# A two-layer diffusion transformer on one core: modulation weights by half tiles over two queues, and layer 1's output product on float16 parts

## The chip, the core and the metric

The kernel runs on one core of a Trainium2 chip as one launch. Its time is the device time of an execution in microseconds (us), and the figure for the kernel before is the median of three runs, 1782.79 us (1778.72 to 1785.88). All five engines are used: TensorE (PE, with its weight loads shown as PEld), VectorE (DVE), ScalarE (ACT), GpSimd (POOL) and SyncE (SP), whose only work here is to issue DMAs. POOL issues DMAs too.

## What is computed

Two layers work on 256 tokens of width 2048 and, in layer 0, on 256 context tokens as well. Layer 0 mixes with a two-dimensional Fourier transform, layer 1 with windowed attention (64 query heads, 8 key heads, context keys in front). Around each branch stands an adaptive normalisation whose shift, scale and gate come from one vector:

```python
for i in range(DEPTH):
    shift, scale, gate = jnp.split((jax.nn.silu(c) @ ada_w[i] + ada_b[i])[:, None, :], 3, axis=-1)
    h = _rmsnorm(x, norm_g[i]) * (1 + scale) + shift
    ...
    y = ...                       # 256 x 4096: Fourier branch, or attention, times silu(z)
    x = x + gate * (y @ w_out[i]) # the output product: 4096 x 2048 weights
    if need_ctx:
        xc = xc + gate_c * (yc @ w_out[i])
return _rmsnorm(x, final_g)
```

Inputs and output are float32. Each operand of a product is split into a high and a low part, and the product is three matmuls.

## The kernel before

**Products.** `mm3` (L144 to L147) issues high times high, high times low and low times high into one bank of PSUM. There are two ways to make the parts. `split` (L65 to L67) copies to float32r on ACT (`S.copy`, L66) and subtracts on DVE (L67); `half_split` does that for half a 1 MB weight tile, and needs two buffers of the pool `ws` (six buffers of 4 KB a partition), one for each part. `split16` (L133 to L138) scales by a power of two into float16 on ACT (L137) and makes the rest on DVE (L138); both parts share one `ws` buffer. The power of two comes from the sum of squares of the whole operand, and is divided out behind the product.

**Order.** Every engine has its own instruction queue and works through it in order. A scheduler puts the instructions of each engine in order when the program is built; `tc.issue_after(x)` tells it that what stands inside must come behind x in that engine's queue. A tile of a pool can be written only when all who use the buffer's earlier tile are done.

**The stages around the change.**
- *z products of layer 0* (about 330 to 670 us): 32 blocks. Beside them run side jobs. `ada_jobs` (L767 on) computes the modulation vectors on DVE with multiply-and-sum instructions over the modulation weights `adw` (L796, each 128x1024, two of them for each half tile, one for layer 1's gate); there are 64 tiles of 1 MB, taken one at a time by `next(ada)`. In this stage each is loaded as two halves, one into `zr` (two buffers) by SP's queue and one into `wa` (a `ws` buffer) by POOL's. `scan_loads` and `scan_sums` (L815 to L825) load layer 0's output weights a first time, in 128x512 pieces by POOL's queue into the pool `act` (33 buffers), and sum their squares on ACT (L817).
- *Output product of layer 0* (about 670 to 1000 us): `for i in range(32)`, two sweeps of 16 steps over 1 MB tiles of `wo0`; a step is 2 weight halves x 8 blocks x 3 = 48 matmuls of 128x512. Steps with kg < 14 use float16 parts. `y_split0` (L868 to L884) makes the float16 parts of y two k at a time: ACT L882, DVE L883. Its output tiles come from the pool `y`, whose 32 buffers hold the 32 y themselves, except the first, which is an `act` tile; so the parts of y number k go into the buffer of y number k-1. In this stage the modulation tiles (38 are left) are loaded whole, into the pool `raw` (three buffers) and by SP's queue, like the tiles of `wo0`. `ada_rate` says how many a step takes: one, two in steps 6 to 9 and 17 to 24, none in 14 to 16 and from 29 on.
- *Keys and values of layer 1* (about 1005 to 1094 us): 8 steps of 48 matmuls on float32r.
- *Attention* (about 1095 to 1620 us): 66 slots (L1430 on). A slot issues the scores of a head pair (`stage_s`: four matmuls, L1359 and L1360; DVE's maximum L1361, ACT's exponential L1364, the float16 probabilities L1376 and L1377, then a DMA transpose by SP's queue), the values of two slots earlier (`stage_o`, L1394 and L1395) and two "units" of projection work from a list: 64 of queries, 64 of z, and at last 12 units ("o") of layer 1's output product, two k-steps each for the first 512 columns. A unit's weights are split one unit ahead. The rotary embedding and some subtractions run on POOL. `y_split` (L1180) splits y for the output product: ACT casts 256 columns, POOL subtracts for k < 24 and DVE for the rest; the parts lie in the 16 buffers of the pool `h1`, which hold the normalised input until the last z unit has read it, and in `act` tiles.
- *The rest of layer 1's output product* (about 1620 to 1770 us): columns 512 to 1535 from `wo1b` and 1536 to 2047 from `wo1c`, all on float32r parts, then gate, residual and the final norm.

Layer 1's output product has 32 k-steps; for each, two token blocks x four chunks of 512 columns x 3 matmuls.

## Time and profile before

| | |
|---|---|
| median of three runs | 1782.79 us (1778.72 to 1785.88) |
| the profiled execution | 1780.77 us |
| its span, first to last instruction | 1779.0 us |
| mean granted TensorE clock | 0.997 |
| HBM read / written | 391.91 MB / 12.59 MB |

The execution that was profiled lies 2.02 us under the median, and 1.77 us of it lie outside the span. In a timeline row the columns are start, length, engine, line and operation, out<-in, and in brackets how long the engine had been idle and what ended that. A row of a group of instructions has count, total, mean length in ns, and then the idle time in front of them. A row of stretches gives, for each, the busy time and the number of instructions of every engine, then the granted clock, the busy share of the 16 DMA engines and GB/s. Matmuls overlap: a row shows one as 0.38 or 0.40 us long, and the pace is the distance between starts.

### The profile page before, as it was taken

To read this page: it belongs to the slowest core of one execution; us is meant where nothing else is said; L and a number is where in the kernel's file an instruction comes from. 1 tells how busy PE (TensorE), PEld (TensorE's weight loads), DVE (VectorE), ACT (ScalarE), POOL (GpSimd) and SP (SyncE) were. 2 spreads that over 40 slices of the span, in tenths; PEclk is the share of its full clock that TensorE was granted. 3 is DMA by queue.
4 is the path that set the end of the run, shared out by engine and by line. 5 is a ranking of instruction groups with operands and counts; after the bars stand their busy time and mean duration, and the time that the engine had idled before them with its cause. 6 is when DMAs were issued, how large, how long until landed. Compare 5 with 4: busy or idle time off the path is not lost. (4 is left out here: it accounts for less than half of the span.)

```text
span 1779.0 us, 26403 instructions
## 1 busy us (share of the span) xinstructions
PE 1740.9 (98%) x9517; PEld 1222.3 (69%) x9517; DVE 1392.8 (78%) x2401; ACT 1062.4 (60%) x1989; POOL 293.3 (16%) x368
## 2 busy tenths in 40 slices
PE   6999999999999999999999999999999999999997
PEld 4679999544444444446444888788878888887886
DVE  5779888797777778876885654899899999997455
ACT  5545556377767747544122533688788878896343
POOL 0002111212222132000000000412303230233010
PEclk9999999999999999999999999999999999999999
DMA  9998998778988989774775323588998897987543
GB/s 394 417 357 247 283 276 237 296 285 319 328 305 317 313 302 322 262 298 171 284 287 222 119 95 115 169 193 208 213 209 199 222 217 203 206 210 264 191 167 142
DMA packets 220962, 438.74 MB, mean 247 GB/s; under 512 B 154720, under 2 KB 155120, under 8 KB 189088
## 3 DMA queue, kind: packets, MB, share of 16 engines
q1 hardware_dynamic: 182784, 351.85, 61.0%
q0 software_dynamic: 33904, 78.25, 14.8%
q10 hardware_dynamic: 4144, 6.95, 1.1%
q8 instruction: 75, 1.23, 0.3%
q14 instruction: 55, 0.45, 0.1%
HBM read 391.91 MB, written 12.59 MB: 227 GB/s over the span
## 5 line engine op out<-in xcount | busy, mean ns | idle before, releaser
L67 DVE TENSOR_TENSOR wl<-raw,wh 128x1024 fp32r<-128x1024 f32 x213 | 282.0, 1329 | 144.5 <-ACT wh L66 129.8
L66 ACT CAST wh<-raw 128x1024 fp32r<-128x1024 f32 x213 | 222.4, 1045 | 177.4 <-PE ps L146 152.7
L146 PE MATMUL ps<-act,wf 128*128 128x512 f16 x512 | 194.0, 379 | 0.0
L145 PE MATMUL ps<-act,wf 128*128 128x512 f16 x512 | 189.8, 379 | 1.4 <-ACT act L864 0.7
L147 PE MATMUL ps<-act,wf 128*128 128x512 f16 x512 | 191.1, 379 | 0.0
L1323 PE MATMUL ps<-h,wh 128*128 128x512 f32 x512 | 184.8, 396 | 0.0
L145 PEld LDWEIGHTS <-wf 128*128 128x128 f16 x960 | 94.0, 98 | 118.0 <-ACT wf L137 7.9
L145 PE MATMUL ps<-y,wf 128*128 128x512 f16 x448 | 170.3, 381 | 3.5 <-ACT wf L137 3.5
L147 PEld LDWEIGHTS <-wf 128*128 128x128 f16 x960 | 93.9, 98 | 113.2 <-DVE wf L138 0.3
L146 PE MATMUL ps<-y,wf 128*128 128x512 f16 x448 | 170.8, 381 | 0.0
L146 PEld LDWEIGHTS <-wf 128*128 128x128 f16 x960 | 94.1, 98 | 109.5 <-issue 1.1
L147 PE MATMUL ps<-y,wf 128*128 128x512 f16 x448 | 164.4, 379 | 0.0
L137 ACT ACTIVATE wf<-raw,nrm 128x1024 f16<-128x1024 f32 x56 | 61.3, 1140 | 139.3 <-DMA raw<-in_wo 133.9
L1325 PE MATMUL ps<-h,wl 128*128 128x256 f32 x512 | 138.6, 281 | 0.0
L146 PE MATMUL ps<-wl,h 128*128 128x512 f32 x320 | 126.8, 396 | 0.2 <-DVE wl L67 0.2
L147 PE MATMUL ps<-wh,h 128*128 128x512 f32 x320 | 125.3, 395 | 0.0
L145 PE MATMUL ps<-wh,h 128*128 128x512 f32 x320 | 124.0, 402 | 0.0
L138 DVE SCALAR_TENSOR_TENSOR wf<-raw,tn,wf 128x1024 f16<-128x1024 f32 x64 | 79.8, 1282 | 42.5 <-ACT wf L137 42.4
L1377 DVE SCALAR_TENSOR_TENSOR f<-p,sm,f 128x512 f16<-128x512 f32 x128 | 105.7, 845 | 9.0 <-ACT f L1376 8.6
L1323 PEld LDWEIGHTS ps<-h,wh 128*128 128x128 f32 x512 | 96.3, 188 | 19.0
L1364 ACT ACTIVATE p<-ps,mx 128x512 f32<-128x512 f32 x128 | 87.9, 689 | 35.4 <-DVE mx L1361 30.6
L1376 ACT ACTIVATE f<-p,sm 128x512 f16<-128x512 f32 x128 | 87.6, 717 | 31.8 <-DMA ft<-f 12.9
(394 smaller groups left out, 4452.1 us busy)
## 6 DMA issues: line engine op xcount, KB each, us to landing
raw<-in_wz SPq DMA_DIRECT2D x64, 1024.0 KB, 5.4
raw<-in_adw SPq DMA_DIRECT2D x38, 1024.0 KB, 6.3
raw<-in_awp SPq DMA_DIRECT2D x32, 1024.0 KB, 12.7
act<-in_wo POOLq DMA_DIRECT2D x128, 256.0 KB, 7.2
raw<-in_wo SPq DMA_DIRECT2D x32, 1024.0 KB, 6.7
raw<-in_wq SPq DMA_DIRECT2D x32, 1024.0 KB, 5.2
raw<-in_wu SPq DMA_DIRECT2D x32, 1016.0 KB, 6.6
raw<-in_wo1b SPq DMA_DIRECT2D x16, 1024.0 KB, 4.9
```

Of the source, the lines that this page charges most:

```text
L66: last_cast[0] = S.copy(h, src).ins
L67: last_sub[0] = eng.tensor_tensor(l, src, h.bitcast(F32), op=ALU.subtract).ins
L137: last_cast[0] = S.activation(w[:, 0], src, AF.Copy, scale=up).ins
L138: last_sub[0] = V.scalar_tensor_tensor(w[:, 1], src, up, w[:, 0], op0=ALU.mult, op1=ALU.subtract).ins
L145: PE.matmul(o, wh, xh, start=start, stop=False)
L146: PE.matmul(o, wh, xl, start=False, stop=False)
L147: return PE.matmul(o, wl, xh, start=False, stop=stop).ins
L1323: PE.matmul(o[0], wh[:, q], hx1[k], start=k == 0, stop=k == KT - 1)
L1325: PE.matmul(o[0][:, 0:N], wl[:, q], hx1[k][:, 0:N], start=False, stop=False)
L1364: S.activation(pt[tb], so[tb], AF.Exp, bias=mx[:, tb : tb + 1], scale=-1.0, accum_out=sm[:, tb : tb + 1])
L1376: S.activation(f[:, 0:512], pt[tb], AF.Copy, scale=sm[:, tb : tb + 1])
L1377: V.scalar_tensor_tensor(f[:, 512:1024], pt[tb], sm[:, tb : tb + 1], f[:, 0:512], op0=ALU.mult, op1=ALU.subtract)
```

## The change

It has four parts, and what each does to the instruction queues is told behind the diff.

```diff
 # ada_jobs
-                            if f == 0 and not out0[0]:
+                            if f == 0:
                                 wf = adat.tile([P, 1024], F32, tag="zr", name="zr", bufs=2)
                                 nc.sync.dma_start(wf, a["adw"][i, kh, fg][:, q])
-                            elif not out0[0]:
+                            else:
                                 wf = wsp.tile([P, 1024], F32, tag="ws", name="wa")
                                 nc.gpsimd.dma_start(wf, a["adw"][i, kh, fg][:, q])
-                            else:
-                                if f == 0:
-                                    w = raw(a["adw"][i, kh, fg])
-                                wf = w[:, q]
 # layer 0's output product
-                        t = (ypool if k else actp).tile([P, 1024], F16, ...)
+                        t = (ypool if k > 1 else actp).tile([P, 1024], F16, ...)
...
+            elif i == 14:
+                scan_sums(); scan_loads1(2)              # both behind last_cast
+            elif 14 < i < 30:
+                with tc.issue_after(last_cast[0]):
+                    scan_tops1()
+                scan_loads1({i: 1 for i in range(17, 25)}.get(i, 2) if i < 29 else 0)
...
             if i in range(1, 31):
-                y_split0(i + 1)
+                with tc.issue_after(last_cast[0]), tc.issue_after(last_sub[0]):
+                    y_split0(i + 1)
...
-            with tc.issue_after(last_sub[0]) if i < 2 or 11 < i < 19 else nullcontext():
+            with tc.issue_after(last_sub[0]):
                 for _ in range(ada_rate.get(i, 1)):
                     next(ada)
 # keys and values: each of 8 steps, behind last_cast / pow_end
+                    scan_tops1()          # S.activation(t, t, AF.Square, accum_out=c) for each tile
+                    scan_loads2(4 if kg < 2 else 3)   # 128x1024 tiles, 4 buffers "pz", POOL's queue
 # layer 1
+            def y_sums(n, i):             # 12 squares of 128x512 on ACT, in slots up to 53
+                    S.activation(act(), y1[j], AF.Square, accum_out=g1[:, 2 + j : 3 + j])
+            def out_sum(): ...            # slot 54
+            def out_scale():              # slot 56: 4 matmuls with one column, 5 small DVE instructions
+            def w_half(t, i):             # half a weight tile as float16 parts in one "ws" buffer
+                w = wsp.tile([P, 2, 1024], F16, tag="ws", name="wf")
+                split16b(w[:, 0], w[:, 1], t[:, i * 1024 : (i + 1) * 1024], uw)
             def y_split(k):
-                if 16 <= k < 24:
-                    t = act(F32R)
-                else:
-                    t = (h1p if k < 16 else fin[0]).tile([P, 512], F32R, ...)
-                split(t[:, 0:N], t[:, N : 2 * N], y1[k // 2][...], GP if k < 24 else V)
+                src = y1[k // 2]
+                if k < 24:                # two k at a time, 512 columns
+                    t = h1p.tile([P, 1024], F16, tag="h1", name="ys", bufs=16)
+                    GP.tensor_tensor(src, src, uy.broadcast_to([P, 512]), op=ALU.mult)
+                    S.copy(t[:, 0:512], src)
+                    GP.tensor_tensor(t[:, 512:1024], src, t[:, 0:512], op=ALU.subtract)
...
+            S.activation(gbc, gbc, AF.Copy, scale=dn1)
-                w = ws_split(raw(a["wo1b"][kg]))
+                w = [(w_half if kg < 12 else half_split)(t, i) for i in range(2)]
```

- **Modulation.** The 38 tiles that layer 0's output product takes are now loaded as two halves, into `zr` by SP and into `wa` by POOL, as in the stage before; `raw` holds `wo0` alone there. In every step, not only in some, the multiply-and-sum instructions come behind the step's weight split.
- **Branch order in layer 0's output product.** `y_split0` comes behind both halves of the step's weight split on ACT and DVE. The first two of its tiles are `act` tiles, so that the parts of y number k go into the buffer of y number k-2.
- **A second scan.** Layer 1's output weights (24 MB) are loaded a first time to sum their squares: 44 pieces of 128x512 in steps 14 to 28 of layer 0's output product, and 26 pieces of 128x1024 in the keys-and-values stage. ACT squares each.
- **Layer 1's output product.** Steps k = 0 to 23 (of 32) use float16 parts in all four column chunks; the other eight stay on float32r and are scaled to match. The weights' parts need one `ws` buffer where they needed two. For y, POOL multiplies 512 columns by the scale, ACT casts them, and POOL subtracts; in POOL's queue all 12 multiplications stand in front of all 12 subtractions. The gate is multiplied by the inverse scale once. In PE's queue the 12 "o" units now stand closer together: behind the scores of slot 60 come 52 of their matmuls in a row, behind those of slot 61 another 46.

More of the change, by code (lines that the diff above doesn't have):

```diff
@@ L825, in scan_loads, with scan_tops1, scan_loads1 @@
                 pend.append((t, j * 2 + q - 64 * (j >= 40)))
+    g1 = gt0.rearrange("p k s -> p (k s)")
+    w1s = [a["wo1a"][i] for i in range(6)] + [a["wo1b"][i] for i in range(12)] + [a["wo1c"][i] for i in range(6)]
+    scans1 = iter(range(48))
+    def scan_tops1():
+        while pend:
+            t, c = pend.pop(0)
+            S.activation(t, t, AF.Square, accum_out=c)
+    def scan_loads1(n):
+        for j in [next(scans1) for _ in range(n)]:
+            for q in range(2):
+                t = act()
+                c = (j % 2 * 2 + q) * 512
+                nc.gpsimd.dma_start(t, w1s[j // 2][:, c : c + 512])
+                k = j * 2 + q
+                k += 80 if k < 28 else -28
+                pend.append((t, scn[:, k : k + 1]))
     def keep(dst, src):
@@ L874, in y_split0 @@
                     if i < 16:
-                        t = (ypool if k else actp).tile([P, 1024], F16, tag="y" if k else "act", name="y")
+                        t = (ypool if k > 1 else actp).tile([P, 1024], F16, tag="y" if k > 1 else "act", name="y")
                         h, l, up = t[:, 0:512], t[:, 512:1024], ysc[:, 1:2]
@@ L1030, in tile_dit @@
                     evac0(sw * 8 + b, o[b])
+    for c, q in ((0, slice(80, 108)), (15, slice(0, 16))):
+        V.tensor_reduce(g1[:, c : c + 1], scn[:, q], axis=AX.X, op=ALU.add)
     x1d = dram.tile([2, P, D], F32, name="x1d")
@@ L1117, in tile_dit, with scan_loads2 @@
                 hc1.append(hc)
+            scn = kvp.tile([P, 26], F32, name="scn", bufs=1)
+            def scan_loads2(n):
+                for j in [next(scans1) for _ in range(n)]:
+                    t = kvp.tile([P, 1024], F32, tag="pz", name="pz", bufs=4)
+                    nc.gpsimd.dma_start(t, w1s[j // 2][:, j % 2 * 1024 : j % 2 * 1024 + 1024])
+                    pend.append((t, scn[:, j - 22 : j - 21]))
             o = [[psum() for _ in range(2)] for _ in range(4)]
@@ new lines, in tile_dit, with out_sum @@
+            ypairs, ynext = [], [0]
+            def y_sums(n, i):
+                while ynext[0] < min(n, len(ypairs)) and ypairs[ynext[0]] <= i - 2:
+                    j = ynext[0]
+                    ynext[0] += 1
+                    S.activation(act(), y1[j], AF.Square, accum_out=g1[:, 2 + j : 3 + j])
+            uw, uy, ub, dn1 = (g1[:, c : c + 1] for c in (20, 21, 22, 23))
+            def out_sum():
+                V.tensor_reduce(g1[:, 14:15], g1[:, 2:14], axis=AX.X, op=ALU.add)
@@ L1433, in tile_dit @@
                     S.copy(ident16[0], ident)
+                y_sums(12, i if i < 54 else 99)
+                if i == 54:
+                    out_sum()
+                if i == 56:
+                    out_scale()
                 if i < 64:
@@ L1477, in tile_dit @@
             for kg in range(16):
-                w = ws_split(raw(a["wo1b"][kg]))
+                t = raw(a["wo1b"][kg])
+                w = [(w_half if kg < 12 else half_split)(t, i) for i in range(2)]
                 for j in range(2):
```

55 lines of the change are left out of this document (43 added, 12 removed).

## The prediction

> **What bounds the kernel now.** I read the page's busy times, then the stretches, then TensorE's timeline wherever a stretch is not full.
>
> ```profile
> PE 1740.9 (98%) x9517; PEld 1222.3 (69%) x9517; DVE 1392.8 (78%) x2401; ACT 1062.4 (60%) x1989; POOL 293.3 (16%) x368
> ```
> ```profile
> 400.00:550.00 150.00, 150.00 (x721) 68.37 (x720) 107.80 (x189) 112.17 (x242) 33.48 (x63) 1.00 0.87 309
> ...
> 850.00:900.00 50.00, 50.00 (x233) 22.67 (x232) 43.90 (x68) 9.37 (x9) 0.00 (x0) 1.00 0.76 293
> ```
> ```profile
> 1005.00:1094.00 89.00, 89.00 (x392) 72.04 (x392) 47.05 (x84) 33.83 (x57) 0.00 (x0) 1.00 0.35 115
> 1100.00:1575.00 475.00, 471.70 (x2563) 392.03 (x2562) 439.45 (x795) 379.82 (x734) 112.59 (x81) 1.00 0.83 204
> 1575.00:1620.00 45.00, 41.57 (x229) 32.71 (x228) 41.99 (x69) 37.40 (x78) 24.59 (x30) 1.00 0.81 223
> 1620.00:1700.00 80.00, 80.00 (x350) 64.96 (x348) 40.68 (x42) 33.46 (x41) 4.22 (x2) 1.00 0.60 210
> ```
>
> TensorE is full in nearly every stretch, at a granted clock of 1.00, so the time is the number of matmuls times their pace, plus a few holes. Only in attention is a second engine near: DVE, 439 of 475 us. Busy is not yet pace; that is read between starts:
>
> ```profile
> 900.05 0.38 PE L146 MATMUL ps<-y,wf 128*128 128x512 f16 x1
> ...
> 903.93 0.38 PE L146 MATMUL ps<-y,wf 128*128 128x512 f16 x1
> ```
> ```profile
> 1640.00 0.40 PE L146 MATMUL ps<-wl,ys 128*128 128x512 f32 x1
> ...
> 1645.60 0.40 PE L146 MATMUL ps<-wl,ys 128*128 128x512 f32 x1
> ```
>
> Between the first two lie 18 matmuls: 3.88 / 18 = 215.6 ns on float16. Between the second two lie 24: 5.60 / 24 = 233.3 ns on float32r, the same shape.
>
> **The change, part by part.**
>
> *Float16 steps.* 24 of 32 steps, 2 blocks x 4 chunks x 3 = 24 matmuls each, are 576; each gets 17.7 ns shorter: 10.2 us. Of these 432 (7.6 us) stand behind attention, where DVE is half idle (40.7 of 80 us) and so is ACT; all of that shows. The other 144 (2.5 us) stand in attention's last slots and show only if DVE keeps up. Splitting costs the same as before: ACT 1140 and DVE 1282 ns a half tile, for 1045 and 1329.
>
> ```profile
> L137 ACT ACTIVATE wf<-raw,tn 128x1024 f16<-128x1024 f32 x64 | 70.0, 1139 | 5.1 <-DVE tn L118 4.0 <-DVE tn L119 1.0
> L138 DVE SCALAR_TENSOR_TENSOR wf<-raw,tn,wf 128x1024 f16<-128x1024 f32 x64 | 79.8, 1282 | 42.5 <-ACT wf L137 42.4
> L67 DVE TENSOR_TENSOR wl<-raw,wh 128x1024 fp32r<-128x1024 f32 x213 | 282.0, 1329 | 144.5 <-ACT wh L66 129.8
> L66 ACT CAST wh<-raw 128x1024 fp32r<-128x1024 f32 x213 | 222.4, 1045 | 177.4 <-PE ps L146 152.7
> ```
>
> The Trainium skill ("TensorE: Matmul & The Clock Gate", section "Wait — 56ns, not 53.3ns?") gives warm matmuls of 512 columns 215.7 ns, without regard to type. The float16 rows agree; the float32r rows do not. By that rule alone this term would be nothing.
>
> *Branch order.* Layer 0's output product has one long hole:
>
> ```profile
> 734.00 0.61 PE L145 MATMUL ps<-y,wf 128*128 128x512 f16 x1 [2.66 <-ACT wf L137]
> 734.40 0.63 PE L146 MATMUL ps<-y,wf 128*128 128x512 f16 x1
> ...
> 737.39 0.40 PE L145 MATMUL ps<-y,wf 128*128 128x512 f16 x1
> ```
> ```profile
> 727.57 0.72 ACT L882 ACTIVATE y<-y,nrm 128x512 f16<-128x512 f32 x1 [2.90 <-DVE y L883]
> 729.11 0.72 ACT L882 ACTIVATE y<-y,nrm 128x512 f16<-128x512 f32 x1 [0.82 <-DVE y L883]
> 730.65 0.72 ACT L882 ACTIVATE y<-y,nrm 128x512 f16<-128x512 f32 x1 [0.82 <-DVE y L883]
> 732.19 0.72 ACT L882 ACTIVATE y<-y,nrm 128x512 f16<-128x512 f32 x1 [0.82 <-DVE y L883]
> 732.82 2.17 ACT L137 ACTIVATE wf<-raw,nrm 128x1024 f16<-128x1024 f32 x2
> ```
>
> ACT casts y in a chain with DVE, since each part goes into the buffer of the y just before it, and the weights wait behind. TensorE is idle for 2.66 us, which with the 0.38 of the matmul before and less one pace is 2.8 us between starts, and then runs eight matmuls in 3.39 us instead of 1.72: 4.5 us in all. The change puts the weights first and one more tile between: 4.5 us go. What is late next is the modulation work on DVE:
>
> ```profile
> L796 DVE CUSTOM_DVE_ANT_0 raw<-raw,cb 128x1024 f32<-128x1024 f32 x76 | 91.0, 1222 | 0.8 <-DMA raw<-in_adw 0.2
> ```
>
> A step has 48 x 0.2156 = 10.35 us, in which DVE is to do two halves (2.6) and up to six multiply-and-sums (7.3), as it did at 43.9 of 50 us without a hole.
>
> *Half tiles.* The same bytes in twice the DMAs. Now `raw` prefetches `wo0` alone, three deep; but POOL's queue holds them among scan loads that wait for `act` buffers, and SP's `zr` loads ahead of `wo0` wait for DVE. From 400 to 550 us the kernel ran in just this form with no hole. I take nothing off and 0.5 us on, bounds -1 to 19 (third rival).
>
> *The second scan.* 70 squares on ACT. In the keys stage 26 of 1.24 us (32 us) fit into ACT's 55 idle us, the 13.6 MB over 89 us raise 115 GB/s to 268. In the product the 44 cost 0.8 us each, beside ACT at 9.4 of 50. The 12 of y in attention (9.6 us in ACT's 95 idle) delay a slot now and then: 0.5 us, bounds 0 to 3.
>
> ```profile
> L817 ACT ACTIVATE act<-act 128x512 f32<-128x512 f32 x128 | 78.7, 616 | 0.0
> L817 ACT ACTIVATION_READ_ACCUMULATOR act<-act 128x1 f32 x128 | 24.1, 189 | 0.0
> L81 ACT ACTIVATE sq<-raw 128x1024 bf16<-128x1024 f32 x52 | 54.2, 1047 | 0.0
> ```
>
> *Attention's end.* POOL had 24 subtractions of 256 columns here, now it has 12 multiplications and 12 subtractions of 512:
>
> ```profile
> 1571.64 15.56 POOL L67 TENSOR_TENSOR ys<-act,ys 128x256 fp32r<-128x256 f32 x15 [0.92 <-ACT ys L66]
> 1605.52 4.24 POOL L67 TENSOR_TENSOR act<-act 128x256 fp32r<-128x256 f32 x4 [18.32 <-ACT act L66]
> ```
> ```profile
> L1162 POOL TENSOR_TENSOR v<-act,v x4: 1351/1420/1612, 1109.5 to 1113.8; 128x512 f16<-128x512 f32 x4
> ```
> ```profile
> gbc<-gated POOLq DMA_DIRECT2D x1, 1024.0 KB, 8.6
> ```
> ```profile
> 1581.07 1.76 DVE L67 TENSOR_TENSOR wl<-raw,wh 128x1024 fp32r<-128x1024 f32 x1
> ...
> 1599.45 1.22 DVE L67 TENSOR_TENSOR wl<-raw,wh 128x1024 fp32r<-128x1024 f32 x1
> ```
>
> POOL's 512 columns took 1.42 us here (1.35 to 1.61). Twelve multiplications, before the first subtraction, are 17 us. They can begin when the scale is out; it comes with the maximum of slot 56, an estimated 5 us behind its scores. A slot is 475 / 64 = 7.4 us, the first "o" matmuls are in slot 59: 3 x 7.4 - 5 = 17 us. So the first subtraction ends some 1.4 us late, less the 0.4 of the two matmuls that need no low part: TensorE waits 1.0 us, bounds 0 to 4 (12 x 1.61 + 1.61 - 17). Behind it a pair takes 1.42 us and its 12 matmuls 2.6. ACT's casts of y wait for the multiplications, and the exponentials of slot 58 stand behind four of them, which are done by then. While POOL works, DVE's subtraction took 1.76 us instead of 1.22, beside it when POOL rests. Nine more us of POOL work (24 x 1.42 for 24 x 1.04), a third of it lost to DVE in this way, cost about 3 us of DVE time; its slack of 7% over 45 us takes two thirds: 1.0 us, bounds 0 to 8. Scale and its four matmuls: 0.2 us. ACT now scales the gate when it has landed, with weight casts behind it; eight halves are cast ahead, 96 matmuls or 20.7 us of cover for the 8.6 us of the load. The holes at attention's very end (45 - 41.6 = 3.4 us) I leave.
>
> *Sum.* 1780.77 - 10.2 - 4.5 + 0.5 + 0.5 + 1.0 + 1.0 + 0.2 = 1769.3 us, made against the profiled execution. This stands 2.0 us under the median of the runs, so the forecast is 13.5 under that.
>
> ```profile
> L1361 DVE CUSTOM_DVE_ANT_0 ps<-ps,mask,nsink x128: 731/752/759, 1139.5 to 1606.7; 128x512 f32<-128x512 f32 x128
> ```
>
> **The rivals.** The row above is DVE's maximum, least, median and longest time.
> 1. *The hole moves.* The order removes the chain between ACT and DVE, but the weights now stand behind multiply-and-sums that wait for `wa`, and TensorE waits as long elsewhere in layer 0's product: 4.5 back, 1773.8. For it: in POOL's queue the modulation halves of the first steps stand behind 21 to 48 scan loads. Against: the z stage, full at 309 GB/s.
> 2. *POOL holds DVE.* 24 instructions of 1.4 us each hold up one DVE subtraction by 0.54 us: 13 us, less 3 of slack, and the closer "o" units leave the last softmax less cover. 7 us more, 1776.3. For it: 1.76 against 1.22. Against: DVE's maximum reads PSUM and never lengthened, and 98 of the matmuls stand ahead of the last two slots. The Trainium skill ("SBUF — State Buffer", section "SBUF: two separate sides") has the port that both share as a lock held for a whole instruction; the rows agree.
> 3. *DMA gives out: slower.* In steps 17 to 24 a step loads 1 MB of `wo0`, 2 of modulation and 0.5 of scan, 3.67 million bytes in 10.35 us: 355 GB/s. It decides from what the 16 engines can do: 309 / 0.87 = 355 at full load. If they give only the 293 of 850 to 900 us, each of eight steps takes 12.5 us and four later ones 10.75: 19 us, 1788.3. Against: scan loads run ahead and need not come in their step.
> 4. *The format doesn't set the pace*; the 233.3 comes from elsewhere. 10.2 back, 1779.5.
>
> **How the numbers follow.** Forecast 0.54, rivals 0.19, 0.16, 0.08, 0.03. Predicted is the forecast's 1769.3. Its costs sum to 3.2; with none, and 3 us of attention's holes (3.3 of 475, 3.4 of 45) closed, it is 1763; the upper end takes in the first two rivals at 1776.3 with the bounds of POOL's wait and of the sums on ACT (3 and 2.5 more, and 1 for DMA) to 1783. A measurement of this kernel tells about 0.5% (8.9 us) from no change, so the limits are 1773.9 and 1791.7. Faster by that: nine tenths of the forecast and half of the first rival, 0.58. Slower by that: half of the third at worse prices, 0.05. Within: 0.37.
>
> **What would show it.** Float16 matmuls of "o" and of `wo1b` at 215.6 ns; no hole over 1 us in layer 0's product; 80 full us behind attention; POOL's 12 multiplications done before the first "o" matmul, within 1 to 2 us. I am wrong if TensorE waits for DVE or for POOL for over 5 us between slots 56 and 61, if a cast waits for `wo0` while TensorE is idle, or if layer 0's product takes over 10.4 us a step.

## The result, and the profile after

The changed kernel takes 1785.24 us (median of 19 runs, 1783.28 to 1787.96), beside 1779.4 us for the kernel before on the same chip (19 runs): a ratio of 1.0033, with a 95% interval of 1.0022 to 1.0044. It is slower by about 5.9 us. Forecast were 1769.3 us, that is 11.5 us under the profiled execution of before and 13.5 us under the median of its three runs, with a range of 1763 to 1783. The result lies above the range, and 5.9 us more instead of 11.5 less is a miss of 17.4 us. The profiled execution took 1783.28 us, its span is 1781.5 us at a mean clock of 0.995.

The first part of the page, and then the stretches that were shown of before (columns as there):

```profile
PE 1733.5 (97%) x9525; PEld 1171.0 (66%) x9525; DVE 1401.8 (79%) x2410; ACT 1128.5 (63%) x2142; POOL 366.4 (21%) x476
```
```profile
850.00:900.00 50.00, 50.00 (x233) 22.68 (x232) 33.40 (x51) 13.98 (x24) 16.13 (x30) 1.00 1.01 387
1005.00:1094.00 89.00, 89.00 (x383) 71.66 (x382) 47.29 (x82) 60.48 (x107) 11.66 (x22) 1.00 0.72 264
1100.00:1575.00 475.00, 468.17 (x2551) 388.02 (x2550) 437.86 (x793) 382.07 (x748) 129.10 (x89) 1.00 0.83 203
1575.00:1620.00 45.00, 33.37 (x147) 15.89 (x147) 37.91 (x54) 31.74 (x58) 22.28 (x20) 0.89 0.73 222
1620.00:1700.00 80.00, 78.31 (x402) 42.38 (x401) 52.56 (x64) 45.39 (x59) 5.03 (x4) 1.00 0.66 220
```

TensorE is busy 7 us less than before, as it should be with shorter matmuls, and yet the span is 2.5 us longer. One stretch stands out: from 1575 to 1620 us TensorE is busy for 33.4 of 45 us, where it was 41.6, at a clock of 0.89 instead of 1.00. The other stretches are nearly full, though from 1100 to 1575 us TensorE has 6.8 us of holes where it had 3.3.

To see where time comes and goes, I take four marks from the starts of matmuls: attention's first scores, the scores of slot 55, the first matmul of the last values (slot 63's), and the end. The first mark is the first start in these rows of the scores' line, of before and of after:

```profile
L1359 PE MATMUL ps<-kkh,qa x64: 389/395/481, 1138.3 to 1597.6; 128*128 128x512 f32 x64
```
```profile
L1440 PE MATMUL ps<-kkh,qa x64: 389/395/582, 1133.0 to 1622.6; 128*128 128x512 f32 x64
```

| stretch, us | before | after | difference | forecast |
|---|---|---|---|---|
| start to first scores | 1138.3 | 1133.0 | -5.3 | -4.0 |
| first scores to slot 55 | 407.0 | 407.9 | +0.9 | +0.5 |
| slot 55 to the last values | 74.3 | 98.4 | **+24.1** | +10.0 |
| the last values to the end | 159.3 | 142.2 | -17.1 | -17.9 |

(The forecast column splits the prediction's terms over the rows. Third row: 44 matmuls of the output product that now stand ahead of the last values, at the old 233.3 ns, 10.3 us, less 2.5 for the 144 that became float16, and 2.2 for waits and the scale. Last row: the same 10.3, and 7.6 for float16.) Three rows came out as forecast within 1.3 us. The whole miss of 14 us between these two traces is in the third.

What TensorE waited for there, by the waits of PE from 1540 to 1645 us in after, and from 1545 to 1625 us in before (us in total, times, longest):

```profile
PE ps L1475 <- DMA ft<-f: 8.5, 1, 8.5
PE ps L146 <- DVE wf L1245: 4.5, 3, 3.8
PE ps L1475 <- ACT ft L1468: 1.7, 1, 1.7
```
```profile
PE ps L1394 <- DVE ft L1387: 1.7, 1, 1.7
PE ps L1394 <- DMA ft<-f: 1.0, 1, 1.0
```

Two waits are new: the very first "o" unit waits for the low part of its *weights* on DVE, and a slot's values wait for their transposed probabilities. PE's timeline at the first:

```profile
1573.28 0.39 PE L145 MATMUL ps<-wf,ys 128*128 128x512 f16 x1
1577.46 0.58 PE L146 MATMUL ps<-wf,ys 128*128 128x512 f16 x1 [3.79 <-DVE wf L1245]
1577.84 0.63 PE L147 MATMUL ps<-wf,ys 128*128 128x512 f16 x1
1578.27 0.63 PE L145 MATMUL ps<-wf,ys 128*128 128x512 f16 x1
...
1580.39 0.38 PE L147 MATMUL ps<-wf,ys 128*128 128x512 f16 x1
```

After the wait the matmuls start 0.43 us apart, half the pace, and the granted clock of 0.89 in the row above shows it too; the wait costs more than its length. The Trainium skill ("TensorE: Matmul & The Clock Gate", section "What's actually happening") has the array at half its clock after an idle window of about 3.4 us, until it has been busy for as long; the trace agrees as to the pace, and the slow stretch here is 2.9 us.

ACT's queue in the same slots shows where the probabilities were:

```profile
1577.26 0.19 ACT L1445 ACTIVATION_READ_ACCUMULATOR p<-ps,mx 128x1 f32 x1
1577.35 0.29 ACT L1446 ACTIVATE es<-mx,sink 128x2 f32<-128x2 f32 x1
1577.53 0.61 ACT L1257 CAST ys<-act 128x512 f16<-128x512 f32 x1
1578.04 2.19 ACT L1244 ACTIVATE wf<-raw,gt 128x1024 f16<-128x1024 f32 x2
1580.13 0.61 ACT L1257 CAST ys<-act 128x512 f16<-128x512 f32 x1
...
1581.35 2.16 ACT L1257 CAST ys<-act 128x512 f16<-128x512 f32 x4
1583.42 0.91 ACT L1263 ACTIVATE ys<-act,gt 128x256 fp32r<-128x256 f32 x2
1584.23 2.18 ACT L1244 ACTIVATE wf<-raw,gt 128x1024 f16<-128x1024 f32 x2
1586.31 1.32 ACT L1457 ACTIVATE f<-p,sm 128x512 f16<-128x512 f32 x2
```

The exponentials are done at 1577.45 us; the slot's float16 probabilities (`f`, L1457) come 8.9 us later, behind six casts of y, two of its last parts and four weight halves, all for units that are due later. Not all of this is ACT's doing: the sums that scale these probabilities were ready only at 1580.7 us, on DVE, so ACT's queue adds 5.6 us. DVE's queue adds 6.4 us: the low part of the same probabilities starts that long after ACT's part, behind two parts of y, a maximum and two weight halves.

```profile
1580.57 0.17 DVE L1448 RECIPROCAL sm<-sm 128x2 f32<-128x2 f32 x1
...
1593.96 0.74 DVE L1458 SCALAR_TENSOR_TENSOR f<-p,sm,f 128x512 f16<-128x512 f32 x1
```

POOL and SP at that time:

```profile
1556.67 16.99 POOL L1256 TENSOR_TENSOR act<-act,gt 128x512 f32<-128x512 f32 x12 [32.11 <-DVE gt L1239]
1573.62 19.34 POOL L1258 TENSOR_TENSOR ys<-act,ys 128x512 f16<-128x512 f32 x12
1592.91 4.38 POOL L1538 DMA_DIRECT2D act<-x1d  x8
```
```profile
1579.53 14.86 SPq L50 DMA_DIRECT2D raw<-in_wo1a  x3
1594.77 9.49 SPq L1460 DMA_TRANSPOSE ft<-f  x2
```

POOL works without a pause for 36 us, and then its queue issues the residual's eight loads 17 us earlier than before (1609.7 there). The next pair of transposes, beside these loads and one weight load, takes 9.5 us in SP's queue, and the first of the two lands 12.4 us after it was issued. And DVE, by groups of instructions from 1556.67 to 1592.95 us (count, total, mean ns), while POOL works:

```profile
L1245 DVE SCALAR_TENSOR_TENSOR wf<-raw,gt,wf 128x1024 f16<-128x1024 f32 x6 | 11.3, 1916 | 0.0
L1458 DVE SCALAR_TENSOR_TENSOR f<-p,sm,f 128x512 f16<-128x512 f32 x4 | 5.2, 1297 | 0.8 <-ACT f L1457 0.8
L1442 DVE CUSTOM_DVE_ANT_0 ps<-ps,mask,nsink 128x512 f32<-128x512 f32 x7 | 5.1, 748 | 0.0
```

The weights' low part takes 1.92 us here for 1.28 in layer 0's product, the probabilities' 1.30 us; the maximum, from PSUM, keeps its 0.75.

### The profile page after: what moved, and what is told of

It reads as the page before. It is cut to its first block, busy times and chain, and to the rows that moved or that the text cites. A ratio compares the mean times of both kernels' runs of the same rounds, so it can differ in the third digit from the quotient of the medians.

```text
span 1781.5 us, 26717 instructions
## 1 busy us (share of the span) xinstructions
PE 1733.5 (97%) x9525; PEld 1171.0 (66%) x9525; DVE 1401.8 (79%) x2410; ACT 1128.5 (63%) x2142; POOL 366.4 (21%) x476
## 5 line engine op out<-in xcount | busy, mean ns | idle before, releaser
L67 DVE TENSOR_TENSOR wl<-raw,wh 128x1024 fp32r<-128x1024 f32 x167 | 218.7, 1311 | 97.8 <-ACT wh L66 76.4
L66 ACT CAST wh<-raw 128x1024 fp32r<-128x1024 f32 x167 | 174.2, 1043 | 94.1 <-PE ps L146 68.3
L790 POOL DMA_DIRECT2D wa<-in_adw x64 | 34.2, 535 | 389.1 <-DVE acc L792 139.4
L1457 ACT ACTIVATE f<-p,sm 128x512 f16<-128x512 f32 x128 | 88.0, 717 | 34.8 <-DMA ft<-f 20.6
```

The costliest lines, as they stand in the source:

```text
L66: last_cast[0] = S.copy(h, src).ins
L67: last_sub[0] = eng.tensor_tensor(l, src, h.bitcast(F32), op=ALU.subtract).ins
L1457: S.activation(f[:, 0:512], pt[tb], AF.Copy, scale=sm[:, tb : tb + 1])
```

## The experiments

Three things are suspected at attention's end: the **order** (units closer together, weight loads ahead of transposes), the **port** (POOL lengthens DVE's instructions) and the **loads** (the residual's, early). A fourth, the **queue** (early work ahead of the softmax on ACT and DVE), was formed last, from the traces of e9 and e13. All runs, with the ratio to the kernel before on the same chip, and two of the stretches. One per cent is 17.8 us. A single execution can differ by some us before attention (e14 and e15 have the same code up to there, and their first scores are at 1132.8 and 1137.5 us), so stretches are compared, not marks. The stretches are those of one execution each, and it need not be a typical one: that of e9 was 5.0 us over its median, that of e16 3.2 under. Up to slot 55 six runs that do the same as after there (e2, e5, e6, e16, e17, e18) range from 405.5 to 408.8 us, so a difference of 2 or 3 us in one stretch tells nothing.

| run | median, us | ratio, 95% | first scores to slot 55 | slot 55 to last values |
|---|---|---|---|---|
| after | 1785.24 | 1.0033 (1.0022 to 1.0044) | 407.9 | 98.4 |
| e1 layer 0 only | 1776.02 | 0.9978 (0.9967 to 0.9988) | 406.0 | 71.9 |
| e2 order held | 1814.53 | 1.0193 (1.0175 to 1.0211) | 407.4 | 131.1 |
| e3 y on DVE | 1778.76 | 0.9989 (0.9979 to 0.9999) | 409.7 | 89.1 |
| e4 e2 and e3 | 1783.89 | 1.0017 (1.0007 to 1.0027) | 407.7 | 99.9 |
| e5 y scaled on ACT | 1789.33 | 1.0064 (1.0042 to 1.0087) | 408.8 | 102.5 |
| e6 residual late | 1782.97 | 1.0022 (1.0009 to 1.0034) | 408.2 | 96.1 |
| e7 scale earlier | 1785.24 | 1.0039 (1.0018 to 1.0059) | 411.8 | 94.5 |
| e8 scale constant | 1783.13 | 1.0022 (1.0007 to 1.0038) | 415.1 | 89.2 |
| e9 no low parts of y | 1772.12 | 0.9960 (0.9941 to 0.9978) | 407.8 | 90.8 |
| e10 float16 behind attention | 1780.27 | 1.0004 (0.9992 to 1.0017) | 410.7 | 76.3 |
| e11 no second scan | 1776.38 | 0.9981 (0.9967 to 0.9996) | 406.7 | 89.3 |
| e12 scan and sums only | 1777.01 | 0.9984 (0.9974 to 0.9995) | 406.6 | 75.3 |
| e13 e9, order held | 1779.08 | 1.0001 (0.9986 to 1.0017) | 413.9 | 90.4 |
| e14 e10, y in pairs | 1773.18 | 0.9970 (0.9959 to 0.9982) | 408.6 | 75.7 |
| e15 e14, 4 sums | 1770.83 | 0.9954 (0.9938 to 0.9969) | 404.7 | 74.6 |
| e16 softmax first | 1776.76 | 0.9979 (0.9965 to 0.9992) | 405.5 | 90.6 |
| e17 e16, e3 and e6 | 1788.50 | 1.0049 (1.0030 to 1.0069) | 407.9 | 102.9 |
| e18 e17, loads later | 1772.22 | 0.9953 (0.9936 to 0.9970) | 407.0 | 86.5 |

**e1: layer 0 alone.** The kernel before with the first two parts of the change.

```diff
-                            if f == 0 and not out0[0]:
+                            if f == 0:
...
-                y_split0(i + 1)
+                with tc.issue_after(last_cast[0]), tc.issue_after(last_sub[0]):
+                    y_split0(i + 1)
```

> The kernel before with the layer 0 part alone (modulation by halves over two queues, branch order); no second scan, layer 1 as before. Both theories of the loss put it in layer 1, so both expect what the markers of the two traces show for layer 0, 5 to 6 us: 1779.4 - 5.5 = 1774 us. If the gain of layer 0 is given back later whatever layer 1 does, it stays at 1779.

3.9 us faster, and from slot 55 on it loses nothing. The gain of layer 0 is real and stays; what the change loses is layer 1's.

**e2: the order held.**

```diff
+                with tc.issue_after(last_pe[0]):
                     filler()
...
+                    with tc.issue_after(trs[-4]) if n < 12 else nullcontext():
                         raw1[0] = raw(a["wo1a"][n // 2])
```

> The changed kernel with the 12 units of the output product inside attention held to two a slot in PE's queue (12 matmuls behind each slot's scores, 12 behind each slot's values), and each load of their weights held behind the transposes of four slots earlier in SP's queue, as in the kernel before. Nothing is computed otherwise. Theory order: the loss at attention's end (holes of some 17 us, against 4 before) comes from the closer order, in which three weight loads stand ahead of a slot's transposes and casts that wait for them stand ahead of the softmax; held, 10 to 13 us come back: 1772 to 1775 us. Theory POOL: POOL's 24 long instructions lengthen DVE's by 13 us in sum wherever the units stand; held, nothing or up to 3 us comes back: 1782 to 1786 us.

29 us slower than the changed kernel: the order theory falls, and not by a little. The probabilities come as late as in after, 8.2 us behind the exponentials in the same slot, and TensorE, with its units held back, has nothing to do meanwhile; it waits for 18 and for 20 us. Undoing the close order does not help, so it is not what costs the time. That the scheduler put the units there to fill the gap that late probabilities leave is a reading that fits. (The edit holds two queues at once, PE's and SP's; e13 below holds PE's alone.)

**e3 and e4: y's parts without POOL**, in the changed kernel's free order and in the held one.

```diff
-                    GP.tensor_tensor(src, src, uy.broadcast_to([P, 512]), op=ALU.mult)
-                    S.copy(t[:, 0:512], src)
-                    GP.tensor_tensor(t[:, 512:1024], src, t[:, 0:512], op=ALU.subtract)
+                    S.activation(t[:, 0:512], src, AF.Copy, scale=uy)
+                    V.scalar_tensor_tensor(t[:, 512:1024], src, uy, t[:, 0:512], op0=ALU.mult, op1=ALU.subtract)
```

> The changed kernel with y's scaled parts made without POOL: ACT scales and casts in one instruction, DVE makes the low part (12 instructions of 128x512, some 0.75 us each, 9 us more on DVE; POOL has none of its 24). The scheduler puts the units still closer together (75 matmuls behind the scores of slot 60, four weight loads in a row in SP's queue). Theory POOL: DVE's instructions keep their short lengths (13 us of lengthening gone, 9 us of work added), and TensorE's holes shrink by 4 us or more: 1781 us or less. Theory order: the order is no better than in the changed kernel, so is the time: 1784 to 1790 us.

> Both: the units held as in e2_order_held, and y's parts without POOL as in e3_y_on_dve. Theory order: within 3 us of e2_order_held, 1770 to 1776 us. Theory POOL: 4 us or more under e2_order_held, and e2 close to the changed kernel: 1778 to 1781 us.

e3 is 7.8 us faster than the changed kernel (0.44%), in spite of 9 us more of DVE work; e4 is 31 us faster than e2. POOL's work is a cause. But the price of the port alone is less certain than 7.8 us, because with POOL's queue empty the residual's loads also move, from 1593 to 1526 us, away from the last transposes:

```profile
1526.45 3.29 POOL L1537 DMA_DIRECT2D act<-x1d  x6
```

Nor is this all of the loss: the stretch is still 89.1 us, where before and the moved matmuls would make 74.3 + 10.3 - 2.5 = 82.1.

**e5, e6, e7, e8: half of POOL's work, the loads, the scale's place.**

```diff
# e5
+                    S.activation(src, src, AF.Copy, scale=uy)
-                    GP.tensor_tensor(src, src, uy.broadcast_to([P, 512]), op=ALU.mult)
# e6
+                    with tc.issue_after(gl):
                         nc.gpsimd.dma_start(x2[tb][c], ...)
# e7
-                if i == 56:
+                if i == 52:
                     out_scale()
# e8
+            for c_, v_ in ((uw, 512.0), (uy, 0.5), (ub, 256.0), (dn1, 2.0**-8)):
+                V.memset(c_, v_)
...
-                if i == 56:
-                    out_scale()
```

> The changed kernel with y's 12 multiplications by the scale on ACT (in place, 12 x 0.6 us) and only the 12 subtractions left on POOL, so POOL's work at attention's end halves, 36 to 19 us; DVE gets nothing new. The scheduler packs the units as close as in the changed kernel or closer. Theory POOL (its instructions lengthen DVE's, which are 13 us too long in sum between 1550 and 1615 us, and everything behind DVE is late): half of the lengthening goes, 5 to 7 us: 1778 to 1780 us. Theory loads (the eight loads of the residual x, 2 MB, which POOL's queue issues as soon as its subtractions are done, 17 us earlier than before, slow the last slots' transposes from 3 to 9 us a pair): they come earlier still, and the time moves by 2 us at most: 1783 to 1787 us.

> The changed kernel with the eight residual loads held in POOL's queue behind the load of the gate, that is behind attention's last scores (about 1626 us, where the changed kernel issues them at 1593 and the kernel before at 1610); every queue's order is otherwise that of the changed kernel. Theory loads: transposes and weight loads keep their short times, the 8.6 us hole shrinks by half or more: 1779 to 1781 us. Theory POOL: the hole is DVE's lateness, nothing changes: 1784 to 1787 us.

> The changed kernel with the sum taken at slot 51 and the scale at slot 52 instead of 54 and 56: the 12 multiplications can run four slots (30 us) earlier, before the last z units end, and only the 12 subtractions fall into the crowded last slots. The work is the same. If what matters is that POOL's burst meets DVE in slots 57 to 61, where DVE has no idle time left (theory POOL, by place): 4 to 6 us come back, 1779 to 1781 us. If DVE loses as much wherever POOL works (theory POOL, by amount), or the loads matter: 1783 to 1787 us.

> The changed kernel with the four scale values written as constants; the second scan, the sums of squares and everything else stay, only the scale's four matmuls and five small DVE instructions are left out. The 12 multiplications then run on POOL one by one as y's blocks come, all over attention. By place: 5 to 8 us come back (the 4 to 6 of an earlier scale and the delay of some 1.7 us at slot 56), 1777 to 1780 us. By amount, or loads: 1782 to 1785 us.

e5 misses both expectations: 5.5 us *slower* than the changed kernel, with half of POOL's work gone. What it added is 12 instructions on ACT, ahead of the casts. That pointed away from POOL alone and to ACT's queue. e6 gives 2.0 us, no more than the two intervals leave open; the loads are a small part here. e7 gives nothing: the stretch behind slot 55 is 3.9 us shorter, and the multiplications, now at 1526 to 1543 us, cost as much in front of it. e8 moves part of the loss ahead of slot 55: 7.2 us longer than after up to there, 9.2 shorter behind. In these two runs the multiplications cost nearly as much in front as they save behind; e11, below, shows that this is not so everywhere.

**e9 and e13: no low parts of y**, in the free and in the held order (PE's queue alone).

```diff
-                    GP.tensor_tensor(src, src, uy.broadcast_to([P, 512]), op=ALU.mult)
-                    S.copy(t[:, 0:512], src)
-                    GP.tensor_tensor(t[:, 512:1024], src, t[:, 0:512], op=ALU.subtract)
+                    S.activation(t[:, 0:512], src, AF.Copy, scale=uy)
-                    yh.extend((t[:, j * N : j * N + N], t[:, 512 + j * N : 512 + j * N + N]) for j in range(2))
+                    yh.extend((t[:, j * N : j * N + N], t[:, j * N : j * N + N]) for j in range(2))
```

> The changed kernel without the low parts of y in the 24 float16 steps: ACT scales and casts y in one instruction (12 x 0.7 us), POOL's 24 instructions and any DVE work for y are left out, and the matmuls with y's low part read the high part instead (as many matmuls as before, the output is another). It shows what attention's end costs without this work. Theory burden (DVE has no idle time in the last slots, so y's low parts cost there about what they take of DVE, by lengthening or by own work): against e3_y_on_dve, which had 9 us of DVE work for them, 6 to 9 us less: 1770 to 1773 us, the forecast. Rival (the loss sits in the closer order, the late scale or the early loads): as e3_y_on_dve, 1776 to 1780 us.

> e9_no_low_parts_of_y (no low parts of y are made; their matmuls read the high part, the output is another) with the 12 units held to 12 matmuls behind each slot's scores and 12 behind each slot's values in PE's queue; SP's queue is left to the scheduler. If what is left at attention's end comes from units that are used up too early and give the last slots no cover: 4 to 6 us less than e9, 1766 to 1768 us. If DVE and ACT simply deliver a slot more slowly than TensorE can take it there, the closer order was what covered this, and holding costs time as in e2 and e4: 1776 us or more.

e9 is where it was expected, at 1772 us, but its stretch is still 90.8 us, no better than e3's: with no work for y's low parts on any engine, 9 us are lost at attention's end, in an execution 5.0 us over the median. Of these, 5.3 us are one wait for the last DMA transposes, which stand beside the loads of the gate and of the final norm's weights (2 MB, from 1610.75 us on); so e9 doesn't show that early work alone costs 9. e13 asks whether units are used up too early. Held, the stretch is the same, 90.4 us, so the order isn't it. In e13's trace more is lost by another thing, ahead of slot 55, in POOL's queue and in PE's:

```profile
1522.83 3.28 POOL L1545 DMA_DIRECT2D act<-x1d  x6
```
```profile
1533.19 0.37 PE L1473 MATMUL ps<-ft,v 128*128 128x256 f16 x1 [4.84 <-DMA ft<-f]
```

With nothing left in POOL's queue, the residual loads are issued at 1523 us, and a slot's transposes wait beside them. e9 has the same loads at 1522.73 us and TensorE waits 1.3 us for transposes there.

**e11, e12, e15: what the scan and the sums cost.** e11 takes both out of e8; e12 adds them, and the scale, to e1, with nothing that uses them; e15 takes 8 of the 12 sums out of e14 (below).

```diff
# e11
-                y_sums(12, i if i < 54 else 99)
...
-                scan_loads1(2)
...
-                    scan_loads2(4 if kg < 2 else 3)
# e15
-                y_sums(12, i if i < 54 else 99)
+                y_sums(4, i if i < 54 else 99)
```

> e8_scale_constant (constant scale values) and also without the second scan of the weights (24 MB of loads, 70 squares on ACT) and without the 12 squares of y in attention; float16 steps and everything else as in the changed kernel. The prediction put the scan and the sums at 0.5 us: then 1782 to 1783 us, within 1.5 us of e8. If the sums delay attention's slots and the loads the stages before, as the markers in the middle of attention suggest (the lead of 6 us behind layer 0 is 4.5 at slot 55): 1779 to 1781 us.

> e1_layer0_only with the second scan, the sums of squares and the scale (slot 56) added, and nothing that uses them: layer 1's output product stays on float32r as in the kernel before. What the preparation of float16 costs by itself. By the markers of the changed kernel (0.8 us lost up to slot 55, 1.8 at the scale): 2 to 3 us over e1's ratio, 1777 to 1779 us. By e8 against e11: 6 to 7 us over e1, 1781 to 1783 us. By the prediction: 0.7 us.

> e14_float16_behind_attention_2 with the squares of 4 of the 12 pairs of y instead of all 12 (the scale is then a coarser estimate of y's size; 8 ACT instructions of 0.8 us fewer in attention). If the sums delay attention's slots by 6 us: 2 to 4 us under e14. If they cost 1 us: within 1.5 us of e14.

By themselves they cost 1.1 us (e12 against e1, 0.06%), no more than the two intervals leave open. Beside e8's POOL work in the same slots they cost 7 us (e8 against e11, whose intervals do not meet). Attention up to slot 55 takes 406.0 us with neither (e1), 406.6 with the sums (e12), 406.7 with POOL's multiplications (e11) and 415.1 with both (e8); only the last stands clear of the spread of single executions. e15 says 2.8 us for eight squares, no more than the two intervals leave open. The cost of such an instruction is not its own: a reading that fits is that it depends on how much slack the slot has left, but that was not measured by itself.

**e10 and e14: float16 behind attention only.** Inside attention all is as before; behind it, y's float16 parts for columns 512 to 2047 are made by ACT and DVE, in e10 in one run, in e14 a pair at a time behind a weight split.

```diff
-                return (w_half if n < 12 else half_split)(raw1[0], n % 2)
+                return half_split(raw1[0], n % 2)
...
                 w = [(w_half if kg < 12 else half_split)(t, i) for i in range(2)]
+                with tc.issue_after(last_cast[0]), tc.issue_after(last_sub[0]):
+                    y_late([kg + 2])
```

> Layer 0 and the second scan as in the changed kernel, but the 12 units inside attention keep the float32r parts and POOL's 24 short subtractions of the kernel before (columns 0 to 511 all on float32r, unscaled); the scale comes at slot 62, and the float16 parts of y are made behind attention by ACT and DVE (12 x 0.7 us each) for columns 512 to 2047, 432 matmuls. Theory burden: nothing new stands in attention's last slots but the sums of squares: 1779.4 - 3.4 (layer 0, as e1_layer0_only measured) - 7.6 (432 x 17.7 ns) + 1 to 3 (scan and sums in attention) = 1769 to 1772 us. Rival (the loss is the scan and the sums, or the float16 pace is lost elsewhere behind attention): 1776 us or more.

> e10_float16_behind_attention with y's float16 parts made one pair at a time, each behind the weight split of two steps earlier, instead of 11 in a row ahead of a weight split that TensorE then waits for (holes of 5 us and slow matmuls behind attention in e10; 160.6 us from the last values to the end). If that was the cause: 152 us from the last values to the end, 7 to 8 us under e10, 1772 to 1774 us. If the float16 pace is lost behind attention in another way: 1777 us or more.

e10 missed: 160.5 us from the last values to the end. In DVE's queue 11 low parts of y, 7.4 us, stood ahead of a weight half that TensorE needed. In pairs (e14) it is 153.8 us and the kernel takes 1773.18 us, faster than before and after. The same fault, work that is not urgent ahead of work that is, and the same cure.

**e16, e17, e18: softmax first.** The queue theory in one edit: what a unit asks for ahead of time on ACT and DVE comes behind the probabilities (`f`) of the slot two before.

```diff
+                    with tc.issue_after(fends[-3][0]), tc.issue_after(fends[-3][1]):
                         return w1_next()
...
+                    with tc.issue_after(fends[-3][0]), tc.issue_after(fends[-3][1]):
+                        while len(yh) <= min(n * 2 + 5, NB - 1) and len(yh) < 28:
+                            y_split(len(yh))
# e18
+                    tick[0] = GP.tensor_tensor(g1[:, 24:25], sm[:, 0:1], sm[:, 0:1], op=ALU.add).ins
...
+                    with tc.issue_after(tick[0]):
                         nc.gpsimd.dma_start(x2[tb][c], ...)
```

> The changed kernel with the weight splits and the parts of y that a unit asks for held, on ACT, DVE and POOL alike as far as these wait for ACT, behind the float16 probabilities of the slot two before; nothing is computed otherwise, POOL keeps its 24 instructions. Theory queue (work made early for later units stands ahead of the softmax in ACT's and DVE's queues): the burst is spread over five slots, the stretch from slot 55 to the last values falls from 98.4 us to 90 or less, 8 us or more come back: 1774 to 1778 us. If only POOL's lengthening counted: 1784 to 1786 us.

> e16_softmax_first with y's scaled parts on ACT and DVE as in e3_y_on_dve (no POOL instruction beside them) and the residual loads held behind attention as in e6_residual_late. Each of the three costs is taken away by itself: queue, port and loads. If they add: the forecast's 1769 us or a little more, 1768 to 1773 us. If DVE has no room for 9 us of y's parts even when they are spread: 1775 us or more.

> e17_softmax_first_no_pool with the loads of the gate and the residual (3 MB) held in POOL's queue behind a one-column POOL addition that reads the last slot's sums, so behind the last transposes that go by DMA. If e17's 13 us hole was the collision of these loads with the last transposes: 10 to 13 us under e17, 1772 to 1776 us, and the stretch from slot 55 to the last values some 90 us or less (102.9 in e17). If the last slots starve for another reason: 1783 us or more.

e16: 9.6 us back (0.54%), with all of POOL's work in place and nothing computed otherwise. Part of it belongs to the other causes: POOL's subtractions now wait for ACT's later casts, so that the residual's loads come at 1611.91 us, 19 us later than in after and behind the transposes. ACT's timeline in e16 at the slot that was shown of after:

```profile
1573.95 0.19 ACT L1449 ACTIVATION_READ_ACCUMULATOR p<-ps,mx 128x1 f32 x1
1574.04 0.28 ACT L1450 ACTIVATE es<-mx,sink 128x2 f32<-128x2 f32 x1
1574.23 1.14 ACT L1244 ACTIVATE wf<-raw,gt 128x1024 f16<-128x1024 f32 x1
...
1578.48 1.33 ACT L1461 ACTIVATE f<-p,sm 128x512 f16<-128x512 f32 x2 [2.41 <-issue]
```

The probabilities follow the exponentials after 4.3 us, not 8.9, and ACT stands idle just before them, since it now waits for DVE's sums alone. e17 was meant to add the other two cures and missed by 15 us. Its POOL and SP queues say why:

```profile
1607.32 3.81 POOL L1544 DMA_DIRECT2D act<-x1d  x7
```
```profile
1607.82 13.44 SPq L1465 DMA_TRANSPOSE ft<-f  x2
```

The loads of gate and residual, held behind attention's last *scores*, fell on the last transposes, which took 13.4 us in SP's queue. In e18 they wait for the last slot's sums, and the same transposes are short:

```profile
1605.34 2.63 SPq L1467 DMA_TRANSPOSE ft<-f  x2
```

1772.22 us, 8.4 us under the kernel before; e15, which keeps float32r inside attention, is as fast. DVE in e18, by groups from 1556 to 1610 us, with POOL at rest:

```profile
L1245 DVE SCALAR_TENSOR_TENSOR wf<-raw,gt,wf 128x1024 f16<-128x1024 f32 x11 | 14.1, 1277 | 0.0
L1463 DVE SCALAR_TENSOR_TENSOR f<-p,sm,f 128x512 f16<-128x512 f32 x12 | 8.8, 748 | 2.4 <-ACT f L1462 2.4
L1257 DVE SCALAR_TENSOR_TENSOR ys<-act,gt,ys 128x512 f16<-128x512 f32 x12 | 8.7, 743 | 0.0
```

Each instruction has its short length, 1277 for 1916 ns and 748 for 1297. Taken against its usual length in the same trace, everything that DVE runs from 1550 to 1620 us is some 13 us too long in sum in after, 7 in before and 1 in e18 (an estimate from the rows of DVE's timelines). So the 8.7 us that y's low parts cost DVE here are less than the lengthening beside POOL's 24 instructions.

## Why the prediction was wrong, step by step

- **Float16's pace: right.** The `wo1b` matmuls run at 215.6 ns: 18 of them lie between these two rows of after, 3.88 us. Behind attention 17.1 us went, where 10.3 for the moved matmuls and 7.6 for float16 make 17.9. Rival 4 is out.

```profile
1660.12 0.38 PE L146 MATMUL ps<-wf,ys 128*128 128x512 f16 x1
...
1664.00 0.38 PE L146 MATMUL ps<-wf,ys 128*128 128x512 f16 x1
```

- **Branch order: right.** ACT casts y in one go behind the weights, and the hole of layer 0 is gone, not moved (rival 1 is out): the last matmul of the first sweep starts at 829.94 us before and at 824.64 after. By e1 the time gained is 3.9 us (2.1 to 5.9), 4.0 were forecast for the two parts.

```profile
829.94 0.39 PE L147 MATMUL ps<-act,wl 128*128 128x512 f32 x1
```
```profile
824.64 0.39 PE L147 MATMUL ps<-act,wl 128*128 128x512 f32 x1
```
```profile
727.68 1.32 ACT L897 ACTIVATE y<-y,nrm 128x512 f16<-128x512 f32 x2
```

- **Half tiles, DMA: right.** From 850 to 900 us the engines gave 387 GB/s, at a busy share of 1.01, and TensorE stayed full. Rival 3 took 293 or 355 GB/s for their limit.
- **The second scan: right in size by itself.** 0.7 us with the scale were forecast, e12 has 1.1 us; beside POOL's work it cost 7 (e8 against e11).
- **Attention's end: the step that failed.** The forecast put POOL's part at 1.0 us for the first subtraction and 1.0 us for DVE, and took DVE's slack of 7% for cover. It was 14 us more in the traces. Three things were wrong in it.
  - *What is made early was priced by the piece, not by its place in a queue.* "Splitting costs the same as before" holds for each half. But a float16 half takes one `ws` buffer where it took two, so twice as many can be split ahead, and all 12 casts of y have a buffer at once. They stood ahead of a slot's probabilities on ACT and on DVE. The forecast counted the halves cast ahead as cover and asked only whether exponentials stand behind casts of y; the wait came behind them. e16 shows the effect of the place: 9.6 us back, with the later loads' part in it. That the freed buffers are why the scheduler chose that place is read from the code, and was not tried.
  - *DVE's lengthening was put too low, and slack set against it that was not there.* The forecast charged 3 us of DVE time for POOL's longer work. While POOL worked, DVE's group rows above say 6 x (1.92 - 1.28) + 4 x (1.30 - 0.75) = 6 us for two kinds of instruction alone; over all kinds it is the 13 us estimated above, as rival 2 had it by 24 x 0.54, but 7 of them were there before, so the change added about 6. DVE has next to no idle time from 1559 to 1602 us in after, so the slack of 7%, which the forecast let take two thirds of the 3 us, was not there. With POOL's work gone 7.8 us come back (e3, the loads' move in it). The first "o" unit did wait, though not for POOL: POOL's first subtraction was done by 1575.3 us, and DVE's 1.94 us weights at 1577.4. The forecast had no term for this wait; in e16, where POOL works on, it is still 3.8 us, in e3 0.5.
  - *A transfer that POOL's work used to hold back was not followed.* With its subtractions done earlier, POOL's queue issued the residual loads 17 us earlier, onto the transposes; 2.0 us by e6, no more than the intervals leave open.
- **Rival 2** had the mechanism by name, POOL holds DVE and the last softmax has less cover, at 7 us and a chance of 0.16. For POOL's part that is close to e3's 7.8; the whole miss is twice as much, since the rival had no term for the queue. The gains cannot be added: e16 gives 9.6 and e3 7.8 us, but both also move the residual's loads. With queue, port and loads all taken away, e18 has 14.2 us (0.80%) back, most of the 17.4 by the medians: its span is 1769.1 us, and the forecast of 1769.3 us for an execution was a span of 1767.5. How the 14.2 us divide among the three is not shown.
- The prediction's own sign, over 5 us of TensorE waiting for DVE or for POOL between slots 56 and 61, was not quite met: for DVE it waited 4.5 us, for POOL not at all. The large wait, 8.5 us, was for DMA transposes behind late probabilities, which the sign did not name.

Open is what sets e18's remaining 4 us against 82.1, and why scan and sums cost so much more beside POOL's multiplications than alone.

## What to carry to other kernels

When a change frees buffers or makes work ready earlier, ask where in each engine's queue that work will now stand, and what with a deadline stands behind it: a burst that fits into an engine's idle time still costs its whole length to the one instruction behind it. Where three engines are nearly full, the average slack may be worth nothing to a burst, as here; price it at full length, and include what it does to the neighbour on the same port. And when a long job leaves a queue, look what that queue issues next, and onto which transfer it falls.

## What the runs showed that was not expected

- DMA transposes suffered more from large loads beside them than the loads did: in SP's queue a pair takes 2.6 us undisturbed (e18), 9.5 us beside 2 MB of residual loads and a weight load (after) and 13.4 us beside the 3 MB of gate and residual (e17). From issue to landing a transpose took 3.0 us at best and 12.4 at worst in after from 1570 to 1640 us; a residual load took 4.9 us in before and 9.2 in after (medians).
- Sums and multiplications, each too cheap in attention to tell from nothing (0.6 and 0.7 us), cost 9 us together (e8).
- After an idle time of 3.8 us six of TensorE's float16 matmuls started 0.43 us apart instead of 0.216, 1.3 us in all, so that this wait cost a third more than its length.
